# Score matmuls on stacked halves, gathers ahead of the dense loop, and three smaller reorderings in a two-block transformer kernel

## The chip, the cores and the metric

The kernel runs on one core of a Trainium2 chip. The metric is the device time of one execution in microseconds (us). The kernel before took 3409.3, 3415.68 and 3416.18 us in three runs, a median of 3415.68.

The engines have short names: PE is TensorE (matmuls), DVE is VectorE, ACT is ScalarE, POOL is GpSimd, SP is SyncE, which here only starts transfers. PSUM holds what PE adds up, SBUF everything else. Each engine runs its own instructions in order. A "FR" matmul is one on fp32r data, the form that PE takes in one pass; an fp32 matmul takes several.

## The reference, cut to what matters

Two blocks run one after the other, each of two layers, width D = 1024, on 256 latent tokens (and, in the first block's first layer, 256 context tokens beside them).

```python
# first block, each layer l:  mix (three branches, one of them attention), then PEER
q = apply_axial_rope(rmsnorm(q, q_norm[l]), ang_row, ang_col)      # 8 heads of 64
k = apply_axial_rope(rmsnorm(k, k_norm[l]), ang_row, ang_col)      # 2 heads of 64
k_all = concat([k, rmsnorm(kc, k_norm[l])])                        # latent and context keys
s = einsum('bqhgd,bkhd->bhgqk', q, k_all) * HEAD_DIM ** -0.5       # the scores
ya = softmax(s) @ v_all

def peer(h):                            # 8 heads, 128 x 128 = 16384 experts
    q = (h @ wq).reshape(C, 8, 2, 128)
    s = einsum('chpd,hpnd->chpn', q, sub_keys)
    s1, i1 = top_k(s[:, :, 0], 16); s2, i2 = top_k(s[:, :, 1], 16)
    top, pos = top_k(all 256 sums s1 + s2, 16)      # 16 experts of each head and token
    g = softmax(top)
    a = gelu(einsum('chkd,cd->chk', u_tab[eidx], h))
    return einsum('chk,chkd->cd', g * a, v_tab[eidx])

# second block, each layer: hybrid mixer, then memory cross attention
log_f = log_sigmoid(f_b + b_forget)     # forget gates: a few columns of the projection
dt    = softplus(dt_c + dt_bias)        # and as few more
xbc   = silu(causal_depthwise_conv(xbc_c, conv_w, conv_b))
```

## The kernel before

**Precision.** Nearly every fp32 operand is split into two fp32r parts, `hi` (an ACT cast, L128) and `lo` (a DVE subtraction of what is left, L129), and a product is three FR matmuls, hi·hi, hi·lo and lo·hi (`mm3`, lines 186 to 188 in the trace). Weights come through SP in tiles `raw` of 512 KB (5 buffers) and are split into `whi` and `wlo` (4 buffers).

**Order.** The code issues instructions in program order to a scheduler that places each engine's instructions by priority. What the engine then runs is a fixed list. `weave` interleaves generators, called units, in program order.

**Mix (L488 on).** For each token tile `qk_unit` norms, rotates and transposes q and k. q stays fp32, in `qT` with two heads of 64 rows on the 128 partitions. k is copied twice into `kT`, once for the upper and once for the lower head of a pair, and the other 64 rows are zeros that POOL wrote. `attn1_unit` then takes for each head one fp32 matmul of 128 queries by 512 keys (256 for the context queries). There are 24 units, each of two heads by 128 queries.

**PEER (L703 on).** All 16384 experts are not gathered for every token. The first 320 tokens in layer 0 (192 in layer 1) are "dense": for each of 128 chunks of 128 experts, `expert_in` multiplies the tokens by the chunk's u rows (24 FR matmuls) and makes G by gelu, a window `win` of routing weights multiplies it to `A`, `A` is split to `Ahl`, and 16 FR matmuls with the chunk's v rows add the result to PSUM. The other 192 (64) tokens are "gathered": for each of the 128 expert slots one indirect DMA brings the u and v rows of one slot for 128 tokens (`gat`, 1 MB, 4 buffers, on POOL's queue), DVE takes the dot product (L896), ACT the gelu (L897), and DVE adds to `gacc` (L908, L910) one gather later. With four buffers a gather waits until the one four ahead of it has been added.

Before the loop: queries and scores (`wq`), then the top 16 of each half and of their sums on DVE, then for each of four (layer 1: two) token tiles `route`, which turns positions into expert numbers `idx` (32 `pr` steps on DVE and PE) and writes the dense weights to DRAM (`wb` to `wd`). A number of `expert_in` run ahead of the loop (13 in layer 0, 30 in layer 1) to keep PE at work during the route. In the loop the n-th gather is placed by this rule:

```python
while gat and done < min(max(c - 5, 0) * ng // 119, ng):   # ng = 192 or 64
    done += 1
    with self.tc.issue_after(dma.ins), self.tc.issue_after(mul.ins):
        next(gat, None)
```

**Hybrid mixer (L1240 on).** First the forget gates and step sizes: a weight of 96 KB (`wfdr`, POOL's queue) is split, 24 matmuls give 24 columns (`fdT`), two transposes and an addition make `fd`. Then twelve `conv_unit`s are woven with the gate projections.

Of the kernel before, what the change touches and what calls it, by code (L numbers as in the profile page):

```python
# [9 lines left out]
F32 = mybir.dt.float32  # L10
# [34 lines left out]
def r3(ap, a):  # L45
    return ap.rearrange("p (a b) -> p a b", a=a)


class Net:
# [369 lines left out]

    def rope(self, out, src, cos, sin, nh, nb, f, pool):  # L420
# [11 lines left out]
        nc.vector.tensor_add(out, out, t[:, :w])  # L432

# [49 lines left out]
    def mix(self, l, both):  # L483
# [3 lines left out]
        with ExitStack() as es:  # L487
# [3 lines left out]
            hT = [ap.tile([128, 8, T], FR, name=n) for n in ("hTh", "hTl")]  # L491
            oT = [ap.tile([128, 4, TB], FR, name=n) for n in ("oTh", "oTl")]
# [4 lines left out]
            qT = bp.tile([128, 4, TB], F32, name="qT")  # L497
            kT = self.k_padded(bp, "kT", T)
            v = bp.tile([128, 4, 128], F32, name="v")
# [114 lines left out]
    def qk_unit(self, tp, rope, ps, t, gi, out, v):  # L614

        nc = self.nc
        cg, sg, kg = rope
        nh = 2 if gi else 8
        s = slice(t * 128, t * 128 + 128)
        q = self.headnorm(ps[:, :nh * 64], nh, tp)  # L620
        r = tp.tile([128, 512], F32, tag="qr", name="qr", bufs=3)[:, :nh * 64]
        if t < 2:
            self.rope(r, q, cg[:, gi, t], sg[:, gi, t], nh, 2, 16, tp)
        else:
            nc.vector.tensor_tensor(r3(r, nh), r3(q, nh), bc(kg[:, gi, None, :], [128, nh, 64]), op=OP.mult)
        if gi:
            self.evac(v[:, t], ps[:, 128:256])
        yield True
        if gi:
            self.k_put(out, r, tp, s)  # L630
            return
# [66 lines left out]
    def peer(self, l, both):  # L698
# [9 lines left out]
        with ExitStack() as es:  # L708
# [22 lines left out]
            with ExitStack() as e2:  # L731
                np_ = self.pool(e2, "wqp", side="right")
                scs, made = {}, []
                for cg in range(5):
                    qT = np_.tile([128, 4, 512], F32, tag="pq", name="pq", bufs=2) if cg < 4 else None
                    for c in range(4 if cg < 4 else 1):
                        if cg < 4:
                            ps = self.psum(c % 2)
                            self.proj_T(ps[:, :T], hT, i["wq"][l, cg * 4 + c], 0, T)
                            nc.scalar.copy(qT[:, c, :T], ps[:, :T])  # L740
                        if c == 0 and cg:
                            for t in range(NT):
                                ps = self.psum()
                                for k in range(4):
                                    nc.tensor.matmul(ps[:, k * 128:k * 128 + 128], pq[:, k, t * 128:t * 128 + 128], keys[:, k],
                                                     start=True, stop=True)
                                sc = scs[cg - 1, t] = np_.tile([128, 512], F32, tag="score", name="score", bufs=8)
                                nc.scalar.copy(sc, ps)
                    pq = qT
                    if cg < 4:  # L750
                        keys = np_.tile([128, 4, 128], F32, tag="keys", name="keys", bufs=2)
                        nc.gpsimd.dma_start(keys, i["keysT"][l, cg])
                    if cg:
                        for t in range(NT):
                            sc = scs[cg - 1, t]
                            for c in range(4):
                                n = (cg - 1) * 4 + c
                                self.top16(np_, sc[:, c * 128:c * 128 + 128], v16[t][:, n], i16[t][:, n], "tk")
                            self.candidates(np_, v16[t], top[t], pos[t], cg - 1)
            with ExitStack() as e2:  # L760
                rp = self.pool(e2, "rt", side="right")
                self.iota128 = rp.tile([128, 128], F32, name="iota128")
                nc.sync.dma_start(self.iota128, i["iota128"])
                self.iotah = rp.tile([128, 16, 8], FH, name="iotah")
                nc.vector.tensor_copy(self.iotah, r3(self.iota128, 16))
                if both:
                    self.mem_kv(0, range(GAPS["peer", 0][1].stop, 16), mp)
                for t in range(NT):
                    self.soft(rp, top[t])
                for t in range(NT):  # L770
                    g0 = (NT - 1 - t) * 128 if t * 128 + 128 > TD else 0
                    self.route(rp, top[t], pos[t], i16[t], t, l, wd, min(max(TD - t * 128, 0), 128), idx[:, g0:], gg[:, g0:])
# [7 lines left out]
            gp = self.pool(es, f"gp{l}", side="right")  # L780
            gat = self.gathered(gp, hT, idx, gg, TD, T) if ng else None
            nb = TD // 16
            ready = {}
            done = 0
            for c in range(128):
# [11 lines left out]
                ready[c] = ahl  # L797
                while gat and done < min(max(c - 5, 0) * ng // 119, ng):
                    done += 1
                    with self.tc.issue_after(dma.ins), self.tc.issue_after(mul.ins):  # L800
                        next(gat, None)
                if c == 125:
                    for _ in gat or ():
                        pass
# [142 lines left out]
    def route(self, rp, top, pos, i16, t, l, wd, nw, idx, gg):  # L947
# [21 lines left out]
        for a in range(2):  # L969
            for j in range(16):  # L970
# [239 lines left out]
    def hybrid(self, l):  # L1210
        nc, i = self.nc, self.i
        with ExitStack() as es:
# [32 lines left out]
            with ExitStack() as ec:  # L1245
                self.gap_fill("hybrid", l)
                self.normT(hT, "nm2T", l, bp)
                pp = self.pool(ec, f"hyp{l}", side="right")

                wr = pp.tile([128, 192], F32, name="wfdr")  # L1250
                nc.gpsimd.dma_start(wr, i["w2fd"][l])
                wf = [pp.tile([128, 192], FR, name=n) for n in ("wfdh", "wfdl")]
                self.split(wr, wf[0], wf[1])
                fdb = self.rowvec(pp, "fd_bias", 24, l)
                ps = self.psum()
                for k in range(8):
                    c = slice(k * 24, k * 24 + 24)
                    self.mm3(ps[:24, :256], (wf[0][:, c], wf[1][:, c]), (hT[0][:, k], hT[1][:, k]), k == 0, k == 7)
                fdT = pp.tile([24, 256], F32, name="fdT")
                nc.scalar.copy(fdT, ps[:24, :256])  # L1260
                for t in range(2):
                    nc.tensor.transpose(ps[:, 256 + t * 24:280 + t * 24], fdT[:, t * 128:t * 128 + 128], self.ident[:24, :24])
                nc.vector.tensor_tensor(fd, r3(ps[:, 256:304], 2), bc(fdb[:, None, :], [128, 2, 24]), op=OP.add)
                gates = self.hybrid_gates(l, hT, gT)
                self.weave((self.conv_unit(l, pp, hT, cw, m, xs, bcT) for m in range(12)), gates)
                for _ in gates:
# [30 lines left out]
            eb.close()  # L1297
        self.dump(f"x2_mix{l}", self.x)

    def hybrid_gates(self, l, hT, gT):  # L1300
# [373 lines left out]
```

## Time and profile before

| | us |
|---|---|
| three runs | 3409.3, 3415.68, 3416.18 |
| profiled execution | 3411.22 |
| its span in the trace | 3409.4 |
| PE busy (share of the span) | 3247.6 (95%) |
| DVE busy | 2598.9 (76%) |
| ACT busy | 1734.0 (51%) |
| POOL busy | 515.9 (15%) |

The stages, from the trace, in us from the span's start: modulation and the first mix to about 486; queries, top-k and route of the first PEER to 786; its dense loop to about 1742; second mix to about 1985; second PEER to about 2755; then hybrid, memory, hybrid, memory and the final norm. "Idle before" in a row is time in which an engine stood still, and the arrow names what ended it. A matmul's own length includes its way through the array, so what one costs is read from the distance between two starts. The granted clock (PEclk) is a share of 2.4 GHz, 0.50 being 1.2 GHz.

### The profile page before, as it was taken

The page shows a single profiled execution, that of the slowest core. Times are in us where ns is not written, and L with a number is a line of the kernel's source. Part 1 is how long each engine was busy: PE and PEld are TensorE (multiplying, and loading weights), DVE is VectorE, ACT ScalarE, POOL GpSimd, SP SyncE. Part 2 cuts the span into 40 slices and gives each one's busy share as a digit, 9 for nine tenths or more (in the row PEclk, how much of TensorE's full clock was granted, in tenths as well). Part 3 has the DMA queues.
Part 4 walks back from the last instruction along what each step waited for, and adds up shares of the span by engine and source line. Part 5 has one row for each costly group of instructions (what it writes and reads, how often), then busy time and mean ns, then how long its engine had stood idle before and what let it go on. Part 6 is the DMA issues. An engine that isn't in the chain of part 4 may idle for free.

```text
span 3409.4 us, 53017 instructions
## 1 busy us (share of the span) xinstructions
PE 3247.6 (95%) x19425; PEld 2779.9 (82%) x19425; DVE 2598.9 (76%) x5429; ACT 1734.0 (51%) x3711; POOL 515.9 (15%) x436
## 2 busy tenths in 40 slices
PE   8999999889999999999999998889999989999998
PEld 5666788768888888888877997769999989889887
DVE  3533449997989888999966678589999967755875
ACT  3443333385444444444444544557777745555554
POOL 0000000112333333333300000122222100000000
PEclk9999999889999999999999998999999999999999
DMA  6556232568999999999945555789999844255433
GB/s 244 193 194 219 88 128 80 173 177 312 377 398 379 378 381 372 379 392 389 390 158 173 166 178 170 267 340 389 372 370 377 346 159 161 93 189 174 142 120 109
DMA packets 196453, 860.52 MB, mean 252 GB/s; under 512 B 23920, under 2 KB 25664, under 8 KB 159712
## 3 DMA queue, kind: packets, MB, share of 16 engines
q1 hardware_dynamic: 141840, 505.94, 41.4%
q0 software_dynamic: 54352, 351.20, 26.8%
q8 instruction: 153, 2.51, 0.3%
q14 instruction: 108, 0.88, 0.1%
HBM read 816.15 MB, written 40.89 MB: 251 GB/s over the span
## 4 chain that ended last, share of the span: by engine, by line
PE 46%; issue 27%; DVE 12%; DMA 8%; POOL 6%; ACT 1%; POOLq 0%; DVEq 0%; SPq 0%; ACTq 0%
PE pf L188 5%; PE pf L186 5%; PE pf L187 5%; PE pf L860 4%; POOL gat L893 4%; PE ps L188 4%; PE ps L187 4%; PE ps L186 4%; DMA gat<-peer_uv,idx 4%; DVE wlo L129 3%; PE ps L824 3%; DVE gacc L910 2%; PE pf L859 2%; PE pf L370 1%; DMA wd<-wb 1%
## 5 line engine op out<-in xcount | busy, mean ns | idle before, releaser
L129 DVE TENSOR_TENSOR wlo<-raw,whi 128x1024 fp32r<-128x1024 f32 x778 | 940.1, 1219 | 388.2 <-ACT whi L128 378.2
L128 ACT CAST whi<-raw 128x1024 fp32r<-128x1024 f32 x778 | 814.4, 1047 | 572.8 <-PE pf L187 193.9
L893 POOL DMA_INDIRECT gat<-peer_uv,idx x256 | 406.2, 1587 | 917.3 <-DVE gacc L910 886.4
L188 PE MATMUL pf<-h2hl,wlo 128*128 128x320 f32 (+2 forms) x1152 | 368.6, 320 | 42.6 <-DVE wlo L129 42.5
L186 PE MATMUL pf<-h2hl,whi 128*128 128x320 f32 (+2 forms) x1152 | 367.2, 319 | 0.4 <-ACT mo L321 0.3
L187 PE MATMUL pf<-h2hl,whi 128*128 128x320 f32 (+2 forms) x1152 | 366.5, 318 | 0.0
L896 DVE SCALAR_TENSOR_TENSOR gat<-gat,h 128x1024 f32<-128x1024 f32 x256 | 311.5, 1217 | 70.2 <-DMA gat<-peer_uv,idx 69.8
L910 DVE SCALAR_TENSOR_TENSOR gacc<-gat,pga,gacc 128x1024 f32<-128x1024 f32 x253 | 322.9, 1276 | 0.0
L187 PE MATMUL ps<-wlo,Ahl 128*128 128x512 f32 x768 | 302.5, 394 | 6.2 <-DVE wlo L129 6.2
L186 PE MATMUL ps<-whi,Ahl 128*128 128x512 f32 x768 | 301.0, 396 | 4.1 <-ACT Ahl L128 4.1
L188 PE MATMUL ps<-whi,Ahl 128*128 128x512 f32 x768 | 301.6, 393 | 0.5 <-DVE Ahl L129 0.5
L188 PEld LDWEIGHTS pf<-h2hl,wlo 128*128 128x128 f32 x1152 | 221.9, 193 | 52.3 <-DVE wlo L129 49.6
L860 PE MATMUL pf<-h2hl,whi 128*128 128x384 f32 x784 | 238.5, 360 | 3.8 <-ACT whi L128 3.6
L186 PEld LDWEIGHTS pf<-h2hl,whi 128*128 128x128 f32 x1152 | 221.3, 192 | 8.1 <-ACT mo L321 0.5
L187 PEld LDWEIGHTS pf<-h2hl,whi 128*128 128x128 f32 x1152 | 221.4, 192 | 7.3
L128 ACT CAST Ahl<-A 128x320 fp32r<-128x320 f32 (+1 forms) x256 | 103.7, 405 | 218.1 <-DVE A L791 213.5
L859 PE MATMUL pf<-h2hl,wlo 128*128 128x192 f32 x686 | 174.9, 255 | 0.0
L188 PEld LDWEIGHTS ps<-whi,Ahl 128*128 128x128 f32 x768 | 145.0, 189 | 33.6 <-DVE Ahl L129 1.0
L187 PEld LDWEIGHTS ps<-wlo,Ahl 128*128 128x128 f32 x768 | 144.9, 189 | 31.0 <-DVE wlo L129 8.7
L186 PEld LDWEIGHTS ps<-whi,Ahl 128*128 128x128 f32 x768 | 144.9, 189 | 27.9 <-ACT Ahl L128 5.4
L897 ACT ACTIVATE pga<-pga 128x1 f32<-128x1 f32 x256 | 51.5, 201 | 226.1 <-DVE gat L896 225.7
L860 PEld LDWEIGHTS pf<-h2hl,whi 128*128 128x128 f32 x784 | 147.6, 188 | 8.6 <-ACT whi L128 4.4
(611 smaller groups left out, 7648.6 us busy)
## 6 DMA issues: line engine op xcount, KB each, us to landing
raw<-peer_uT SPq DMA_DIRECT2D x256, 512.0 KB
raw<-peer_v SPq DMA_DIRECT2D x256, 512.0 KB
raw<-ada_w SPq DMA_DIRECT2D x96, 512.0 KB
wd<-wb POOLq DMA_DIRECT2D x32, 1024.0 KB, 6.8
raw<-w_g SPq DMA_DIRECT2D x48, 512.0 KB
win<-wd POOLq DMA_DIRECT2D x16, 1280.0 KB, 9.5
raw<-wq SPq DMA_DIRECT2D x32, 512.0 KB
raw<-w2o SPq DMA_DIRECT2D x32, 512.0 KB
```

The costliest lines, as they stand in the source:

```text
L128: nc.scalar.copy(hi, src)
L129: nc.vector.tensor_sub(lo, src, hi.bitcast(F32))
L186: mm(ps, ah, bh, start=start, stop=False)
L187: mm(ps, ah, bl, start=False, stop=False)
L188: self.last = mm(ps, al, bh, start=False, stop=stop).ins
L824: nc.tensor.matmul(acc[nd][n], ahl[:, 2 * TD - part:], v[e][:, n], start=b == 0 and e == 0, stop=b == 127 and e == 1)
L859: mm(src, u[1][:, k], h2[:, k, 0, :TD], start=False, stop=False)
L860: self.last = mm(r3(ps[:, :2 * TD], 2), u[0][:, k], h2[:, k, :, :TD], start=k == 0, stop=k == 7).ins
L893: nc.gpsimd.indirect_dma_start(out=uv.rearrange("p a b -> p (a b)"), out_offset=None, in_=i["peer_uv"], in_offset=bass.IndirectOffsetOnAxi ...
L896: nc.vector.scalar_tensor_tensor(uv[:, 0], uv[:, 0], 1.0, h2, op0=OP.mult, op1=OP.mult, accum_out=a[:, 0:1])
L897: nc.scalar.activation(a[:, 1:2], a[:, 0:1], AF.Gelu_apprx_tanh)
L910: self.nc.vector.scalar_tensor_tensor(acc, uv[:, 1], a[:, 1:2], acc, op0=OP.mult, op1=OP.add)
```

## The change

There are five parts.

1. **Stacked scores.** q is duplicated before its transpose, so that each head stands twice on the 128 partitions; the upper 64 rows become the hi part, the lower 64 the lo part (one ACT copy that rounds, one DVE subtraction on the lower half). k is duplicated too and split into `kTh` and `kTl`. A score is then two FR matmuls, with kTh and with kTl, in place of one fp32 matmul. Eight heads need eight transposes where four pairs needed four. The attention's output takes qT's place, and the zeros of `kT` are gone.
2. **Queries and scores of layer 1** are all placed ahead of the top-k; layer 0 keeps its order.
3. **Softmax** over the 16 weights moves from ahead of all routes into each route, behind its `pr` steps.
4. **Early gathering, layer 0.** The gather's buffers open ahead of the `expert_in`s; six gathers are placed among the thirteen, and the other 186 are spread from chunk 2 to 124 where 192 stood from 5 to 124.
5. **Forget gates** become a unit that is joined to the third convolution.

```diff
-            for hh in range(2):  # attn1_unit
-            nc.tensor.matmul(ps[hh][:, :nk], qT[:, j, q0:q0 + 128], kT[:, hh, g, k0:k0 + nk], start=True, stop=True)
+            for n, k in enumerate(kT):
+                nc.tensor.matmul(ps[hh][:, :nk], qT[:, 2 * j + hh, q0:q0 + 128], k[:, g, k0:k0 + nk], start=n == 0, stop=n == 1)
...
-        pt = self.psum(True)  # qk_unit
-        for j in range(4):
-            nc.tensor.transpose(pt[:, j * 128:(j + 1) * 128], r[:, j * 128:(j + 1) * 128], self.ident)
-        self.evac(out[:, :, s], r3(pt, 4))
+        n = min(nh, 4)
+        for h0 in range(0, nh, n):
+            pt = self.psum(not gi)
+            for h in range(n):
+                nc.tensor.transpose(pt[:, h * 128:h * 128 + 128], r[:, h0 + h].rearrange("p a b -> p (a b)"), self.ident)
+            pt = r3(pt[:, :n * 128], n)
+            if gi:
+                self.split(pt, out[0][:, :, s], out[1][:, :, s])
+            else:
+                o = out[:, h0:h0 + n, s]
+                nc.scalar.copy(o, pt)
+                nc.vector.tensor_sub(o[64:128], pt[64:128], o[64:128].bitcast(F32))
...
+                made = [scores(cg) for cg in range(4)]  # peer
...
+                    if cg and both:
+                        best(cg - 1)
+                if not both:
+                    for cg in range(4):
+                        best(cg)
...
-                for t in range(NT):
-                    self.soft(rp, top[t])
...
-            gs = [self.expert_in(lp, l, c, h2, h32, TD, c < WHOLE[l]) for c in range(ahead)]
+            gp = self.pool(es, f"gp{l}", side="right")
+            gat = self.gathered(gp, hT, idx, gg, TD, T) if ng else iter(())
+            gs, g0 = [], 0
+            for c in range(ahead):
+                gs.append(self.expert_in(lp, l, c, h2, h32, TD, c < WHOLE[l]))
+                if both and c % 2:
+                    next(gat, None)
+                    g0 += 1
...
-            done = 0
+            done, c0 = g0, 2 if both else 5
-                while gat and done < min(max(c - 5, 0) * ng // 119, ng):
+                while done < min(g0 + max(c - c0, 0) * (ng - g0) // (124 - c0), ng):
...
+        self.soft(rp, top)  # route, behind the pr loop
...
+                us = [self.conv_unit(l, pp, hT, cw, m, xs, bcT) for m in range(12)]  # hybrid
+                us[2] = self.joined(self.fd_unit(l, pp, hT, fd), us[2])
+                self.weave(us, gates)
```

How the fixed lists move is read from the built programs.

POOL's queue at the end of layer 0's route, before (wd is the routing weights' write, win a window of them, gat a gather):

```order
L1032 DMA wd_3682<-wb 128x16x128 x12
L788 DMA win<-wd_3682 128x2560
L893 DMA gat<-peer_uv,idx 128x2048 x3
L788 DMA win<-wd_3682 128x2560
L893 DMA gat<-peer_uv,idx 128x2048
L788 DMA win<-wd_3682 128x2560
L893 DMA gat<-peer_uv,idx 128x2048 x13
```

and after:

```order
L1065 DMA wd_3735<-wb 128x16x128 x12
L925 DMA gat<-peer_uv,idx 128x2048 x6
L820 DMA win<-wd_3735 128x2560
L925 DMA gat<-peer_uv,idx 128x2048 x3
L820 DMA win<-wd_3735 128x2560
L925 DMA gat<-peer_uv,idx 128x2048 x6
L820 DMA win<-wd_3735 128x2560
L925 DMA gat<-peer_uv,idx 128x2048 x12
```

The first window now stands behind six gathers and the second behind nine, and each later window has 12 or 13 gathers before the next, where nearly all had 13.

DVE behind the expert numbers of the last routed tile (idx), before:

```order
L993 CAST idx<-ef 128x128
L129 TENSOR_TENSOR wlo<-raw,whi 128x1024 x3
L791 TENSOR_TENSOR A<-G,win 128x320
L129 TENSOR_TENSOR wlo<-raw,whi 128x1024
...
L887 TENSOR_TENSOR hs<-h2hl 128x128 x2
L129 TENSOR_TENSOR wlo<-raw,whi 128x1024
L896 SCALAR_TENSOR_TENSOR gat,pga<-gat,h_7874 128x1024 x3
```

and after:

```order
L1026 CAST idx<-ef 128x128
L919 TENSOR_TENSOR hs<-h2hl 128x128 x8
L928 SCALAR_TENSOR_TENSOR gat,pga<-gat,h_7448 128x1024
L129 TENSOR_TENSOR wlo<-raw,whi 128x1024
L940 TENSOR_SCALAR gacc<-gat,pga 128x1024
...
L928 SCALAR_TENSOR_TENSOR gat,pga<-gat,h_7448 128x1024
L942 SCALAR_TENSOR_TENSOR gacc<-gat,pga,gacc 128x1024
L129 TENSOR_TENSOR wlo<-raw,whi 128x1024
L823 TENSOR_TENSOR A<-G,win 128x320 x2
```

Before, thirteen splits of weights (wlo) and eight products with windows (A) stood ahead of the first gather's use; now six gathers are used ahead of the first product with a window, each with a split behind it. On PE the matmuls of `expert_in` that stand behind the route's last matmul grow from 186 to 264.

PE at the start of the first hybrid mixer, before (wfdh and wfdl are the forget gates' weights, h3h and h3l the normed tokens):

```order
L262 MATMUL ps<-dg,x 128x128 x13
L186 MATMUL pf<-h3h,whi 128x256
...
L188 MATMUL pf<-h3h,wlo 128x256
L186 MATMUL ps<-h3h,wfdh 24x256
L187 MATMUL ps<-h3l,wfdh 24x256
L186 MATMUL ps<-h3h,whi 128x256
L188 MATMUL ps<-h3h,wfdl 24x256
```

and after:

```order
L262 MATMUL ps<-dg,x 128x128 x13
L186 MATMUL ps<-h3h,whi 128x256
...
L1220 MATMUL ps<-ident,cacc 128x128 x2
L186 MATMUL pf<-h3h,whi 128x256
...
L186 MATMUL ps<-h3h,wfdh 24x256
L187 MATMUL ps<-h3l,wfdh 24x256
L188 MATMUL ps<-h3h,wfdl 24x256
L186 MATMUL ps<-h3h,whi 128x256
```

Before, 24 matmuls of a gate stood between the normed tokens and the forget gates; now 48 of two gates, 48 of two convolutions and two transposes stand there.

## Rows read from the trace of the kernel before

**Rows 1.** The page: engines in 40 slices, tenths busy; DMA is 16 engines' share.
```profile
PE   8999999889999999999999998889999989999998
...
DMA  6556232568999999999945555789999844255433
```
**Rows 2.** Timeline of PE in the first mix: start, us, engine, line, operation, operands, count.
```profile
211.05 0.40 PE L188 MATMUL pf<-hTh,wlo 128*128 128x512 f32 x1
211.28 0.39 PE L186 MATMUL pf<-hTh,whi 128*128 128x512 f32 x1
...
219.96 1.98 PE L645 MATMUL ps<-kT,qT 128*128 128x512 f32 x4
221.88 1.09 PE L660 MATMUL ps<-pT,v 128*64 128x128 f32 x16
```
**Rows 3.** The score line L645: all its matmuls, min/median/max ns, first and last start.
```profile
L645 PE MATMUL ps<-kT,qT x96: 379/592/697, 137.4 to 1888.7; 128*128 128x512 f32 x64, 128*128 128x256 f32 x32
```
**Rows 4.** Timeline of PE in the second mix.
```profile
1830.92 0.66 PE L634 MATMUL pf<-ident,qr 128*128 128x128 f32 x4
...
1854.99 0.28 PE L188 MATMUL pf<-hTh,wlo 128*128 128x256 f32 x1
1855.11 0.29 PE L186 MATMUL pf<-hTh,whi 128*128 128x256 f32 x1
```
**Rows 5.** Windows of both mixes: stretch, us, PE, PEld, DVE, ACT, POOL busy, PEclk, DMA share, GB/s.
```profile
120.00:130.00 10.00, 9.20 (x52) 6.47 (x50) 8.29 (x27) 4.32 (x14) 0.00 (x0) 1.00 0.30 103
1860.00:1880.00 20.00, 20.00 (x170) 17.01 (x167) 12.24 (x31) 14.46 (x30) 0.00 (x0) 1.00 0.35 106
```
**Rows 6.** DVE's copies of a transposed q tile in the first mix.
```profile
L121 DVE COPY qT<-pf x4: 684/690/692, 112.7 to 125.1; 128x512 f32<-128x512 f32 x4
```
**Rows 7.** The page's group of DVE's split subtraction: busy us, mean ns, idle before.
```profile
L129 DVE TENSOR_TENSOR wlo<-raw,whi 128x1024 fp32r<-128x1024 f32 x778 | 940.1, 1219 | 388.2 <-ACT whi L128 378.2
```
**Rows 8.** Windows of layer 0's route, its dense loop, and the loop's start.
```profile
650.00:786.00 136.00, 113.45 (x986) 84.99 (x985) 124.29 (x319) 108.59 (x272) 26.26 (x26) 0.86 0.64 190
...
850.00:1700.00 850.00, 815.53 (x4463) 734.15 (x4462) 775.58 (x1002) 404.22 (x922) 294.41 (x195) 0.99 0.98 383
...
816.00:846.00 30.00, 30.00 (x135) 24.22 (x134) 25.41 (x42) 14.96 (x34) 8.39 (x6) 1.00 0.76 293
```
**Rows 9.** Transfers in 850 to 1700: issues, KB each, median us to landing.
```profile
raw<-peer_v SPq DMA_DIRECT2D x113, 512.0 KB
...
gat<-peer_uv,idx POOLq DMA_INDIRECT x182, 9.4
```
**Rows 10.** Waits in 850 to 1700: who for whom, us in total, times, longest.
```profile
POOL gat L893 <- DVE gacc L910: 534.2, 178, 7.6
...
PE pf L188 <- DVE wlo L129: 33.7, 19, 4.1
```
**Rows 11.** Timeline of PE over one chunk of the dense loop, v matmuls to v matmuls.
```profile
1004.43 0.40 PE L186 MATMUL ps<-whi,Ahl 128*128 128x512 f32 x1
...
1011.19 0.31 PE L186 MATMUL pf<-h2hl,whi 128*128 128x320 f32 x1
...
1011.63 0.40 PE L186 MATMUL ps<-whi,Ahl 128*128 128x512 f32 x1
```
**Rows 12.** Timeline of POOL's queue: the fifth gather of layer 0.
```profile
833.17 1.69 POOL L893 DMA_INDIRECT gat<-peer_uv,idx  x1 [7.76 <-DVE gacc L908]
```
**Rows 13.** Timeline of PE at the first hybrid mixer.
```profile
2776.18 0.41 PE L186 MATMUL ps<-h3h,wfdh 128*24 128x256 f32 x1 [3.65 <-ACT wfdh L128]
```
**Rows 14.** The same place on ACT.
```profile
2775.78 0.35 ACT L128 CAST wfdh<-wfdr 128x192 fp32r<-128x192 f32 x1 [4.67 <-DMA wfdr<-w2fd]
```
**Rows 15.** Windows: behind that place, and among layer 1's top-k.
```profile
2776.00:2782.00 6.00, 5.82 (x28) 4.52 (x29) 1.58 (x2) 3.00 (x5) 0.00 (x0) 0.50 0.68 249
...
2046.00:2052.00 6.00, 1.29 (x9) 1.09 (x9) 6.00 (x32) 1.32 (x2) 0.00 (x0) 0.97 0.00 0
```
**Rows 16.** A wait of DVE behind layer 1's route.
```profile
DVE A L791 <- DMA win<-wd: 16.4, 1, 16.4
```

More of the change, by code (lines that the diff above doesn't have):

```diff
@@ L418, in headnorm, with rope @@
         return qn[:, :w]
-    def rope(self, out, src, cos, sin, nh, nb, f, pool):
+    def rope(self, out, src, cos, sin, nh, nb, f, pool, add=None):
         nc = self.nc
@@ L491, in mix @@
             hT = [ap.tile([128, 8, T], FR, name=n) for n in ("hTh", "hTl")]
-            oT = [ap.tile([128, 4, TB], FR, name=n) for n in ("oTh", "oTl")]
+            qT = ap.tile([128, 8, TB], FR, name="qT")
+            oT = [qT.rearrange("p (j n) t -> p n j t", n=2)[:, n] for n in range(2)]
             pscale = ap.tile([128, 2], F32, name="pscale")
@@ L496, in mix @@
             bp = self.pool(eb, f"mixb{l}")
-            qT = bp.tile([128, 4, TB], F32, name="qT")
-            kT = self.k_padded(bp, "kT", T)
+            kT = [bp.tile([128, 2, T], FR, name=n) for n in ("kTh", "kTl")]
             v = bp.tile([128, 4, 128], F32, name="v")
@@ L732, in peer @@
                 np_ = self.pool(e2, "wqp", side="right")
-                scs, made = {}, []
-                for cg in range(5):
[L735 to L741, printed above, removed]
-                            for t in range(NT):
[L743 to L749, printed above, removed]
+                scs = {}
@@ new lines, in scores @@
+                def scores(cg):
+                    qT = np_.tile([128, 4, 512], F32, tag="pq", name="pq", bufs=2)
+                    keys = np_.tile([128, 4, 128], F32, tag="keys", name="keys", bufs=2)
+                    nc.gpsimd.dma_start(keys, i["keysT"][l, cg])
+                    for c in range(4):
+                        ps = self.psum(c % 2)
+                        self.proj_T(ps[:, :T], hT, i["wq"][l, cg * 4 + c], 0, T)
+                        nc.scalar.copy(qT[:, c, :T], ps[:, :T])
+                        yield
+                    for t in range(NT):
+                        ps = self.psum()
+                        for k in range(4):
+                            nc.tensor.matmul(ps[:, k * 128:k * 128 + 128], qT[:, k, t * 128:t * 128 + 128], keys[:, k],
+                                             start=True, stop=True)
+                        sc = scs[cg, t] = np_.tile([128, 512], F32, tag="score", name="score", bufs=8)
+                        nc.scalar.copy(sc, ps)
@@ L750, in peer, with best @@
+                def best(cg):
+                    for t in range(NT):
+                        sc = scs[cg, t]
+                        for c in range(4):
+                            n = cg * 4 + c
+                            self.top16(np_, sc[:, c * 128:c * 128 + 128], v16[t][:, n], i16[t][:, n], "tk")
+                        self.candidates(np_, v16[t], top[t], pos[t], cg)
+                made = [scores(cg) for cg in range(4)]
+                for cg in range(5):
                     if cg < 4:
-                        keys = np_.tile([128, 4, 128], F32, tag="keys", name="keys", bufs=2)
@@ L752, in peer @@
-                        nc.gpsimd.dma_start(keys, i["keysT"][l, cg])
+                        next(made[cg])
                     if cg:
[L754 to L759, printed above, removed]
+                        for _ in made[cg - 1]:
+                            pass
@@ L760, in peer @@
+                    for _ in range(3 if cg < 4 else 0):
+                        next(made[cg])
+                    if cg and both:
[3 more added lines that the diff above has]
+                        best(cg)
             with ExitStack() as e2:
@@ L768, in peer @@
                 for t in range(NT):
-                    self.soft(rp, top[t])
-                for t in range(NT):
                     g0 = (NT - 1 - t) * 128 if t * 128 + 128 > TD else 0
@@ L802, in peer @@
                 if c == 125:
-                    for _ in gat or ():
+                    for _ in gat:
                         pass
@@ L1248, in hybrid @@
                 pp = self.pool(ec, f"hyp{l}", side="right")
[L1250 to L1263, printed above, removed]
                 gates = self.hybrid_gates(l, hT, gT)
-                self.weave((self.conv_unit(l, pp, hT, cw, m, xs, bcT) for m in range(12)), gates)
+                us = [self.conv_unit(l, pp, hT, cw, m, xs, bcT) for m in range(12)]
+                us[2] = self.joined(self.fd_unit(l, pp, hT, fd), us[2])
+                self.weave(us, gates)
                 for _ in gates:
@@ L1298, in hybrid, with joined, fd_unit @@
         self.dump(f"x2_mix{l}", self.x)
+    @staticmethod
+    def joined(a, b):
+        next(a, None)
+        yield from b
+        for _ in a:
+            pass
+    def fd_unit(self, l, pp, hT, fd):
+        nc, i = self.nc, self.i
+        wr = pp.tile([128, 192], F32, name="wfdr")
+        nc.gpsimd.dma_start(wr, i["w2fd"][l])
+        wf = [pp.tile([128, 192], FR, name=n) for n in ("wfdh", "wfdl")]
+        self.split(wr, wf[0], wf[1])
+        fdb = self.rowvec(pp, "fd_bias", 24, l)
+        ps = self.psum()
+        for k in range(8):
+            c = slice(k * 24, k * 24 + 24)
+            self.mm3(ps[:24, :256], (wf[0][:, c], wf[1][:, c]), (hT[0][:, k], hT[1][:, k]), k == 0, k == 7)
+        fdT = pp.tile([24, 256], F32, name="fdT")
+        nc.scalar.copy(fdT, ps[:24, :256])
+        yield True
+        for t in range(2):
+            nc.tensor.transpose(ps[:, 256 + t * 24:280 + t * 24], fdT[:, t * 128:t * 128 + 128], self.ident[:24, :24])
+        nc.vector.tensor_tensor(fd, r3(ps[:, 256:304], 2), bc(fdb[:, None, :], [128, 2, 24]), op=OP.add)
     def hybrid_gates(self, l, hT, gT):
```

17 lines of the change are left out of this document (8 added, 9 removed).

## The prediction

> **What bounds the kernel now.** I read the page first, then one stretch for each part of the change. The page [rows 1] shows two regimes. In most slices PE is at 9 tenths with DMA at 2 to 6; there a microsecond off PE is a microsecond off the end. In the dense loop of layer 0 PE and DMA both stand at 9, and which of them ends it decides what early gathering is worth.
>
> In both mixes PE is never short of work once the attention runs: 20.00 of 20 us busy at a granted clock of 1.00, with DVE at 12.24 and ACT at 14.46 [rows 5]. Only where q and k are made are PE (9.20 of 10) and DVE (8.29) both nearly full.
>
> In the dense loop one chunk takes PE 7.20 us from v matmuls to v matmuls when it does not wait (1011.63 − 1004.43) [rows 11]. There were 113 chunks in 850 us by the v issues [rows 9], so a chunk took 7.52. The 33.7 us that PE waited for split weights [rows 10] are most of the difference. DMA is at 0.98 for those 850 us, moving 383 GB/s [rows 8]. So transfers pace the loop, and PE keeps some 0.3 us in a chunk, about 36 us over the loop, in reserve. That gathers wait 534.2 us for gacc [rows 10] is the closed ring of four buffers, not a lack of DVE time (775.58 of 850).
>
> **Part 1, scores.** One unit of the 512-key kind takes 221.88 − 219.96 = 1.92 us for two heads [rows 2]. It becomes four FR matmuls of 512 columns at 211.28 − 211.05 = 0.233 us, 0.93 together: 0.99 saved. A 256-key unit has half the columns: 0.96 for two heads, against four matmuls of 0.12 (1855.11 − 1854.99) [rows 4], 0.48 saved. The 64 long and 32 short records [rows 3] are four to a unit, 16 and 8 units. 16 × 0.99 + 8 × 0.48 = 19.7 us less on PE, 12 in the first mix and 8 in the second.
>
> Added on PE: six q tiles with four more transposes each. Four took at most 0.66 us [rows 4], so 24 × 0.145 = 3.5 us (0.145 between that row's two bounds, 0.11 and 0.165). Net −16.2.
>
> The transposes run in a stretch whose granted clock is 1.00 [rows 5], the upper level. The Trainium skill, "TensorE: Matmul & The Clock Gate", section "Part 4: PE-mode transpose", says that a transpose doesn't count as PE activity the way a matmul does, and gives about 275 ns in one kernel's context. By that figure the 24 would cost an estimated 6.6 us and this part would be −13.1; the spacing in this trace is half of it and stands.
>
> Added on DVE, for each of the six q tiles: the last rope step (or the gain) writes 1024 columns in place of 512, and two subtractions from PSUM on 64 partitions take the place of one copy of 512 columns. With 0.69 us for a 512-column operation [rows 6] and 1.219 for 1024 [rows 7] that is 0.53 + 0.69 = 1.2 us a tile, 7.3 in all. For k, the doubling is paid by the copy that goes. DVE has 1.7 us of 10 free there [rows 5]. If all shows, part 1 is −8.9; if none, −16.2. I take a quarter, since DVE's 8.29 leaves it room but its order is fixed: **−14.4**.
>
> **Part 5, forget gates.** PE stands still for 3.65 us because ACT's cast of wfdh ended last [rows 13], and the cast waited 4.67 us for its 96 KB [rows 14]. Behind the pause the granted clock is 0.50: 28 matmuls took 5.82 us [rows 15], 0.208 each in place of 0.12, 2.5 lost. The 48 gate and 48 convolution matmuls that now stand in front are 96 × 0.12 = 11.5 us of work with weights that have their own buffers, so the 96 KB are there in time. Next late is nothing I can see: the conv's splits were ready before. −3.65 − 2.5 = **−6.2**; the bounds are 0 (another weight late in its place) and −7.
>
> **Part 4, early gathering.** Three effects.
> First, three `expert_in`s' ACT and DVE work (each a gelu, a cast, a subtraction) leaves the route, where DVE is busy 124.29 of 136 us and ACT 108.59 [rows 8]. 3 × 1.2 us of DVE splits [rows 7] make the route about 3 us shorter.
> Second, their 78 matmuls at 0.147 us ((1011.63 − 1011.19) / 3) [rows 11], 11.5 us, now come behind the route. PE's reserve of about 36 us swallows that if transfers still end the loop.
> Third, the transfers. From 816 to 846 DMA stands at 0.76 [rows 8], so 30 × 0.24 = 7.2 us idle: the fifth gather waits until 833.17 for the first to be added [rows 12]. With the gathers used ahead of A, most of that fills; I take 5. Against it, two u tiles fewer have been loaded by the route's end, 1.05 MB at 383 GB/s, 2.7 us. Bytes in all are the same: 3 + 5 − 2.7 gives **−5**. The bounds: −10 if the whole idle time goes and the u tiles cost nothing; +8.5 if PE's 11.5 shows in full against the route's 3.
>
> The Trainium skill, "DMA: Bandwidth & Descriptors", section "Anatomy of one DMA — SWDGE (gpsimd) path", fits a transfer to 2.0 us and 436 GB/s. By it, as an estimate, a chunk's 2.88 MB (383 GB/s × 7.52 us) pass in 6.6 us, under PE's 7.20; PE would end the loop and the sum would be the first rival's. The trace disagrees: 383 GB/s at a share of 0.98, and 9.4 us from issue to landing of a gather.
>
> **Parts 2 and 3.** Layer 1's PE has 1.29 busy us in 2046 to 2052 [rows 15], where a query's weight split stood among the top-k on DVE; ten splits come earlier now. But DVE is full there (6.00 of 6), the top-k keeps its length, and behind the route a window's load is last (16.4 us) [rows 16]. So what PE gains becomes waiting. The softmax only moves, in layer 0 to a place where DVE and ACT are as busy; in layer 1 it comes ahead of the casts that the routing waits for, 1 to 2 us late. **−1** for both, bounds −4 and +4.
>
> **Sum.** −14.4 − 6.2 − 5 − 1 = −26.6 on the profiled 3411.2 gives 3384.6. That execution lies 4.5 us under the median of its three runs (3415.7) and 1.9 above the fastest; between them I say **3386 us**. By the ends the sum runs from −37 to +4.
>
> **Rivals.**
> *PE ends the loop.* DMA's 0.98 would be a queue that is always full, not a ceiling. For it: PE is busy 815.53 of 850 us [rows 8]. Against: it waited for weights all the same [rows 10]. Then part 4 is +8.5, the rest stands: −13, **3399**.
> *The loop falls to PE's pace.* Gathers per chunk go from 192/119 = 1.61 to 186/122 = 1.52, 0.09 MB less, at 383 GB/s 0.24 us a chunk; if the early gathers cost nothing, 112 × 0.24 = 27 us go, a chunk takes 7.28, near PE's 7.20. For it: 0.24 of idle share at the loop's start. Against: that is 7 us of room, and six gathers of 1.05 MB need 16. Then part 4 is about −25: −46, **3366**.
> *Slower: DVE stands before early gathers.* A gather needs 9.4 us to land [rows 9]; its use now stands on DVE ahead of a weight split that PE needs. With four split buffers PE has 4 × 3.5 = 14 us of work in hand at the route's end, so the first wait hides; but the fifth and sixth gather start only when the first and second have been added, and land 9.4 us later. If each of the six holds PE, and half the clock follows each pause as in rows 15, six times 5.5 us is 33. It decides from there, 33 against the 26.6: **3424**. Against it: each stall also lets transfers run ahead, and the reserve swallows 36.
> *The score doesn't gain*, because softmax on DVE and ACT sets the attention's pace: against it stand 12.24 and 14.46 of 20 [rows 5]. Then −12, near the first rival, **3400**.
>
> **How the numbers follow.** My forecast has 0.56; PE ending the loop 0.15, the score without gain 0.07, PE's pace 0.13, slower 0.09. The likeliest one's own range, with the bounds of its unknowns half used, is 3374 to 3398. The range for 8 in 10 takes in PE's pace and both middle rivals with their spread: 3363 to 3407. A measurement of this kernel can tell 0.2%, 6.8 us, from no change. Faster: the forecast, PE's pace, and most of the two middle rivals, 0.82. Within: the rest of those, 0.10. Slower: 0.08.
>
> **What would show it.** Right: L657 in place of L645 with four matmuls in about 0.93 us and the second mix some 7 us shorter; no pause at the first wfdh, its window at 1.00; in 816 to 846 a DMA share of 0.9; a loop that ends some 5 us earlier against the route's start, DMA still at 0.98. Wrong: in the loop PE without waits (first rival); DMA's share falling under 0.95 (second); PE idle several times between the route's end and the first A, with DVE's gat waiting for its DMA (third); DVE at 10 of 10 while q is made and PE standing beside it (part 1 at its upper bound).

## The result and the profile after

The changed kernel takes 3371.97 us (median of four runs, 3367.91 to 3373.43) where the kernel before takes 3414.68: a ratio of 0.9876, 95% interval 0.9859 to 0.9893, 42.7 us less. The forecast was 3386 us, 26.6 less on the profiled execution; the time lies in its range of 3363 to 3407. The profiled executions differ by 3411.22 − 3371.84 = 39.4 us, and the stages show where. One execution of spread_only below, at 5407.1 us and a mean granted clock of 0.645, is left out of that kernel's ratio.

Three marks cut the span: the last expert numbers of layer 0 (idx), and the updates of x behind the mixes (upd) and behind the dense loops (gat). For each instruction group the rows give ns min/median/max and the first and last start; the first start of upd and of gat belongs to layer 0, the last to layer 1. Before:

```profile
L584 DVE TENSOR_TENSOR x<-x,upd x8: 681/682/692, 444.6 to 1987.5; 128x512 f32<-128x512 f32 x8
L837 DVE TENSOR_TENSOR x<-x,gat x8: 682/688/694, 1743.1 to 2757.4; 128x512 f32<-128x512 f32 x8
```
```profile
L993 DVE CAST idx<-ef x1: 216/216/216, 786.2 to 786.2; 128x128 int32<-128x128 f32 x1
```

and after:

```profile
L589 DVE TENSOR_TENSOR x<-x,upd x8: 684/685/693, 436.6 to 1955.7; 128x512 f32<-128x512 f32 x8
L869 DVE TENSOR_TENSOR x<-x,gat x8: 681/688/695, 1718.5 to 2722.4; 128x512 f32<-128x512 f32 x8
```
```profile
L1026 DVE CAST idx<-ef x1: 226/226/226, 778.8 to 778.8; 128x128 int32<-128x128 f32 x1
```

The first mix ends 8.0 us earlier (444.6 to 436.6). From there to the expert numbers nothing is won: 341.6 us before, 342.2 after. The dense loop of layer 0 takes 939.7 us (778.8 to 1718.5) in place of 956.9, 17.2 less. The second mix takes 237.2 in place of 244.4, 7.2 less. Layer 1's PEER is 3.2 us shorter, and what follows it 4.3 (span 3370.1 against 3409.4).

The page's slices, after, answer to [rows 1]:

```profile
PE   8999999879899999999999997989999999999998
...
DMA  6566232569999999999944555889999854255432
```

The picture is the same: PE and the transfers at 9 in the dense loops, PE with the transfers well below it elsewhere. What changed shows only in rows with finer numbers.

The scores gain a little less than computed. The timeline of PE in the first mix, after, answers to [rows 2]:

```profile
176.44 0.50 PE L657 MATMUL ps<-kTh,qT 128*128 128x512 f32 x1
176.78 0.39 PE L657 MATMUL ps<-kTl,qT 128*128 128x512 f32 x1
177.00 0.39 PE L657 MATMUL ps<-kTh,qT 128*128 128x512 f32 x1
177.23 0.39 PE L657 MATMUL ps<-kTl,qT 128*128 128x512 f32 x1
177.55 1.09 PE L672 MATMUL ps<-pT,v 128*64 128x128 f32 x16
```

A unit goes from 1.92 us to 177.55 − 176.44 = 1.11: the first of the four stands 0.34 from the second, not 0.23, and the next instruction 0.32 behind the last. In the second mix a unit goes from 1.81 (1850.63 to 1852.44) to 1.03 (1823.43 to 1824.46), and a 256-key unit of the first from 1.06 (262.38 to 263.44) to 0.66 (244.58 to 245.24).

The dense loop is where the forecast was small. These are the windows 900 to 1650 (us, then busy us and instructions of PE, PEld, DVE, ACT, POOL, PEclk, DMA share, GB/s), the issues of v tiles and gathers in them, and before's one wait of PE there. Before:

```profile
900.00:1650.00 750.00, 720.98 (x3955) 649.87 (x3954) 684.49 (x885) 358.10 (x817) 260.45 (x172) 0.99 0.98 385
```
```profile
raw<-peer_v SPq DMA_DIRECT2D x99, 512.0 KB
gat<-peer_uv,idx POOLq DMA_INDIRECT x160, 9.2
```
```profile
PE pf L188 <- DVE wlo L129: 29.0, 16, 4.1
```

After:

```profile
900.00:1650.00 750.00, 750.00 (x4143) 674.16 (x4142) 693.98 (x897) 380.21 (x836) 264.94 (x169) 1.00 0.99 390
```
```profile
raw<-peer_v SPq DMA_DIRECT2D x104, 512.0 KB
gat<-peer_uv,idx POOLq DMA_INDIRECT x157
```

In the same 750 us there are 104 chunks in place of 99, 7.21 us each, which is PE's own pace of [rows 11]; PE waits for nothing. DMA's share is 0.99 against 0.98, but it moved 390 GB/s against 385. So a chunk took 2.92 MB before and 2.81 MB after; by these two rates, as an estimate, the fewer bytes account for 0.27 of the 0.36 us that a chunk got shorter, and the higher rate for the rest.

What PE's waits hung on is seen on DVE, which makes the split weights: before, it stood still for 65.5 of the 750 us, nearly all of it ahead of gathers that had not landed. After, that wait is a third, though DVE did more work (693.98 us for 684.49). Before and after:

```profile
DVE gat L896 <- DMA gat<-peer_uv,idx: 60.9, 33, 6.1
```
```profile
DVE gat L928 <- DMA gat<-peer_uv,idx: 17.7, 15, 2.4
```

The loop's start filled up too: 816 to 846 had 293 GB/s at 0.76 [rows 8]; the same window has 396 GB/s at 1.00 after, where the forecast's sign was a share of 0.9. Two windows around it, after:

```profile
810.00:840.00 30.00, 30.00 (x160) 26.51 (x160) 28.35 (x39) 16.53 (x40) 7.21 (x6) 1.00 1.01 414
840.00:870.00 30.00, 24.66 (x108) 19.95 (x108) 25.59 (x37) 12.27 (x30) 10.30 (x8) 0.94 0.91 352
```

Behind the filled stretch PE stands for 5 of 30 us. That is not a price of the early gathers: the kernel before stands about as long in the same window.

```profile
840.00:870.00 30.00, 25.27 (x119) 21.33 (x118) 27.86 (x38) 13.13 (x33) 10.34 (x8) 0.95 0.95 349
```

POOL's timeline, after, shows how the six are issued, against [rows 12]:

```profile
779.89 1.07 POOL L925 DMA_INDIRECT gat<-peer_uv,idx  x1 [3.87 <-PE pf L920]
...
790.11 1.97 POOL L925 DMA_INDIRECT gat<-peer_uv,idx  x1 [4.68 <-DMA gat<-peer_uv,idx]
794.00 1.67 POOL L925 DMA_INDIRECT gat<-peer_uv,idx  x1 [1.92 <-DVE gacc L942]
795.68 0.61 POOL L820 DMA_DIRECT2D win<-wd  x1
```

The fifth gather starts at 790.1, 11.3 us behind the expert numbers, where it started 47 us behind them (833.17 − 786.2).

### The profile page after: what moved, and what is told of

It reads as the page before. It is cut to its first block, busy times and chain, and to the rows that moved or that the text cites. A ratio compares the mean times of both kernels' runs of the same rounds, so it can differ in the third digit from the quotient of the medians.

```text
span 3370.1 us, 53059 instructions
## 1 busy us (share of the span) xinstructions
PE 3230.3 (96%) x19449; PEld 2775.4 (82%) x19449; DVE 2607.3 (77%) x5430; ACT 1748.3 (52%) x3720; POOL 519.6 (15%) x432
## 5 line engine op out<-in xcount | busy, mean ns | idle before, releaser
L925 POOL DMA_INDIRECT gat<-peer_uv,idx x256 | 413.8, 1616 | 918.8 <-DVE gacc L942 875.2
L186 PE MATMUL pf<-h2hl,whi 128*128 128x320 f32 (+2 forms) x1152 | 362.7, 315 | 0.2 <-ACT mo L321 0.2
L187 PE MATMUL pf<-h2hl,whi 128*128 128x320 f32 (+2 forms) x1152 | 361.8, 314 | 0.0
L187 PE MATMUL ps<-wlo,Ahl 128*128 128x512 f32 x768 | 305.4, 398 | 10.5 <-DVE wlo L129 10.4
L856 PE MATMUL ps<-wlo,Ahl 128*128 128x512 f32 x384 | 151.4, 397 | 0.0
```

Source lines behind the costliest of these rows:

```text
L186: mm(ps, ah, bh, start=start, stop=False)
L187: mm(ps, ah, bl, start=False, stop=False)
L856: nc.tensor.matmul(acc[nd][n], ahl[:, 2 * TD - part:], v[e][:, n], start=b == 0 and e == 0, stop=b == 127 and e == 1)
L925: nc.gpsimd.indirect_dma_start(out=uv.rearrange("p a b -> p (a b)"), out_offset=None, in_=i["peer_uv"], in_offset=bass.IndirectOffsetOnAxi ...
```

## Experiments

All were profiled. The times are medians against the kernel before on the same chip. They scatter more than the stages do, so the stages are set side by side first (us, from each profile, cut at the same marks; "behind" is all that follows layer 1's last gather update):

| | first mix | to idx | dense loop 0 | second mix | PEER 1 | behind |
|---|---|---|---|---|---|---|
| before | 444.6 | 341.6 | 956.9 | 244.4 | 769.9 | 652.0 |
| changed | 436.6 | 342.2 | 939.7 | 237.2 | 766.7 | 647.7 |
| changed_again | 437.9 | 343.0 | 940.2 | 239.0 | 766.3 | 647.7 |
| b_only_scores | 437.4 | 341.8 | 959.2 | 239.4 | 767.1 | 649.8 |
| a_gathers_undone | 436.4 | 343.7 | 959.5 | 238.1 | 774.8 | 648.4 |
| a_softmax_undone | 435.3 | 343.0 | 944.7 | 240.5 | 772.6 | 649.4 |
| a_gates_undone | 435.6 | 344.4 | 943.0 | 239.8 | 767.3 | 649.2 |
| queries_undone | 436.5 | 343.2 | 940.9 | 238.7 | 766.4 | 647.8 |
| spread_only | 435.6 | 347.3 | 944.0 | 237.7 | 770.1 | 649.7 |
| early_only | 434.8 | 343.3 | 948.1 | 239.6 | 768.8 | 647.5 |
| early_twelve | 436.8 | 346.9 | 958.1 | 237.9 | 768.2 | 647.9 |
| before_24_fewer | 447.4 | 343.4 | 909.0 | 242.4 | 764.9 | 646.9 |
| changed_24_fewer | 437.1 | 343.4 | 933.3 | 239.3 | 764.8 | 648.4 |
| paced_gathers | 436.7 | 346.5 | 939.8 | 239.5 | 767.9 | 651.8 |

PEER 1 goes from 764.8 to 774.8 among kernels whose code for it hardly differs. Its 3.2 us of the result are not told from scatter. The stage "to idx" goes from 341.6 to 347.3; where it is longer, PE can do work in it that would else stand in the loop, so two loops are compared safely only with that stage taken in.

**b_only_scores.** The kernel before with the diff's hunks on `rope`, `mix`, `qk_unit` and `attn1_unit` alone.

```diff
-            nc.tensor.matmul(ps[hh][:, :nk], qT[:, j, q0:q0 + 128], kT[:, hh, g, k0:k0 + nk], start=True, stop=True)
+            for n, k in enumerate(kT):
+                nc.tensor.matmul(ps[hh][:, :nk], qT[:, 2 * j + hh, q0:q0 + 128], k[:, g, k0:k0 + nk], start=n == 0, stop=n == 1)
```

> The kernel before with part 1 alone (stacked scores). My theory, by the starts of the stages in the two traces (first mix 8.0 us shorter, second mix 7.2): about 15 us faster than before, 3399 to 3401. Rival: the shorter mixes come partly from other parts (the order of layer 1's queries, the pools), and part 1 alone gives under 10. Second rival: what PE saves there is lost again in the dense loop of layer 0, where transfers pace the work and start no earlier: then only the second mix's 7 are left.

3403.41 us, ratio 0.997 (0.9956 to 0.9985): 9.5 us by the medians, 14.7 by the spans of the profiled pair. The medians fall short of the 3399 to 3401 expected, and their interval, 5 to 15 us, does not separate the theory from its first rival; the stages do. The mixes are 7.2 and 5.0 us shorter with part 1 alone, and the dense loop is not (959.2). Part 1 gives some 12 us here, at its place, and the second rival, that the dense loop takes the first mix's gain back, is not borne out beyond the 2 us by which that loop is longer.

**a_gathers_undone.**

```diff
-                if both and c % 2:
-                    next(gat, None)
-                    g0 += 1
...
-            done, c0 = g0, 2 if both else 5
+            done, c0 = g0, 5
```

> The changed kernel with part 4 undone (gathers as before: none ahead of the loop, 192 from chunk 5 to 124). Theory: part 4 alone is the 17 us by which layer 0's dense loop got shorter, so 3387 to 3391, PE waits for split weights in the loop again (30 us or more) and a chunk takes 7.5 us again. Rival: the loop got shorter because parts 1 to 3 let it start in another state; then under 8 us are lost.

3397.87 us, ratio 0.9955 (0.9942 to 0.9968), 7 us slower than the 3387 to 3391 expected. The dense loop is back at 959.5, and PE's wait is back:

```profile
PE pf L188 <- DVE wlo L129: 27.1, 15, 3.6
```

With b_only_scores that gives three loops without part 4 (956.9 to 959.5) and five with it (939.7 to 944.7). Part 4 is worth 12 to 20 us there, 17 in the result's pair, and no other part brings it.

**a_softmax_undone.** `soft` again ahead of all routes.

```diff
+                for t in range(NT):
+                    self.soft(rp, top[t])
...
-        self.soft(rp, top)
```

> The changed kernel with part 3 undone (softmax of all tiles ahead of all routes). Theory: the softmax only moves within a stretch where DVE is full, so no difference that can be told, within 3 us of 3372. Rival: it is what made layer 1's route 1.8 us longer, so this version is 2 us faster; or what made room at the top-k's end, then it is 3 us slower.

3381.53 us, ratio 0.9896 (0.9872 to 0.9921). Against the changed kernel's 0.9876 and (changed_again) 0.9896 it can't be told apart; layer 0's way to the expert numbers is unchanged (343.0). Inconclusive for a microsecond or two, as the forecast's size was.

**a_gates_undone.**

```diff
-                us[2] = self.joined(self.fd_unit(l, pp, hT, fd), us[2])
```
(and the forget gates ahead of the convolutions as before)

> The changed kernel with part 5 undone (forget gates ahead of the convolutions). Theory: the pause of 3.7 us and the half clock behind it come back, 5 us slower in the first hybrid mixer, and the second mixer gains 0.8 us: 3376 to 3378. Rival: the pause was a matter of when the dense loop ended against POOL's queue and SP's loads; in the changed kernel the 96 KB come in time all the same and nothing is lost.

3379.67 us, ratio 0.9904 (0.9879 to 0.9929), not told apart by time; the stage behind PEER 1 is 1.5 us longer than in the changed kernel, where 5 were expected. That is within the scatter of this stage among kernels that all have part 5 (647.5 to 651.8). The pause is back, but not what I had priced behind it. PE's timeline at the forget gates:

```profile
2748.26 0.30 PE L186 MATMUL ps<-h3h,wfdh 128*24 128x256 f32 x1 [3.22 <-ACT wfdh L128]
2748.39 0.28 PE L187 MATMUL ps<-h3l,wfdh 128*24 128x256 f32 x1
```

The matmuls stand 0.13 apart, not 0.21: the granted clock stayed at 1.00. In b_only_scores (pause 3.37) and before_24_fewer (3.43) it stayed there too. Only in the profiled execution of before (3.65) [rows 13, 15] was it at 0.50.

**changed_again, spread_only, early_only, early_twelve**, together on another chip.

> The changed kernel once more, beside the next three on one chip: 3372, within 5 us; layer 0's dense loop (from the last expert numbers to the first update of x) 937 to 946 us.

3378.66 us, ratio 0.9896 (0.9881 to 0.9911); the loop takes 940.2. The time is 1.7 us above the range expected, and the whole change is worth 37.1 us here, where the result had 42.7.

```diff
-                if both and c % 2:
+                if both and c < 0:      # spread_only
```

> The changed kernel without the six early gathers: all 192 spread from chunk 2 to 124 (1.57 a chunk, in place of six and 1.52). Theory (what counts is the megabytes moved in the first 60 us behind the route, where DMA was idle): most of part 4's gain goes, the dense loop takes 951 to 957 us and PE waits for split weights through the whole loop. Rival (the lower number of gathers per chunk is enough to bring the loop to PE's pace of 7.20): the loop stays under 946.

3386.21 us, ratio 0.9913 (0.9898 to 0.9929). By the loop alone the rival, under 946: 944.0. But the way to the expert numbers is 5.7 us longer than before (347.3 for 341.6). Both stages together take 1291.3, against 1298.5 before and 1281.9 in the changed kernel: starting at chunk 2 in place of 5, with fewer gathers a chunk (1.57 for 1.61), brings 7 of 17 us, and PE's wait in 900 to 1650 falls to half:

```profile
PE pf L188 <- DVE wlo L129: 13.5, 12, 2.5
```

```diff
-            done, c0 = g0, 2 if both else 5
+            done, c0 = g0, 5      # early_only
```

> The changed kernel with the six early gathers but the others from chunk 5 on as before (1.56 a chunk). Theory (early megabytes): about half of the gain is kept, the dense loop takes 945 to 950 us. Rival (the spread matters): 953 or more.

3378.62 us, ratio 0.9888 (0.9873 to 0.9904). 948.1, as my theory had it, with 10.1 us of that wait. With the stage ahead of it, 1291.4: 7 of 17 us again. So by the stages each half brings about half, though by the medians there is no difference between this kernel and the changed one (3378.66); what the later start adds to the six is not shown in the time.

```diff
-                if both and c % 2:
+                if both and c:          # early_twelve
```

> The changed kernel with twelve early gathers, one behind each of the thirteen expert_ins but the first, in place of six. Theory (PE's pace of 7.20 a chunk now ends the loop): nothing more to gain, the dense loop takes 937 to 946 us and DMA's share falls a little towards the loop's end. Rival (transfers still end it): 6 x 2.7 = up to 16 us more gained. Second rival (DVE stands before gathers that haven't landed, and the windows' products behind it): slower, 950 us or more, with PE idle between the route's end and the first v matmul.

3388.69 us, ratio 0.9924 (0.991 to 0.9937). The second rival, which is also my forecast's way to slower: 958.1, all of part 4's gain lost. The first window is issued behind the twelfth gather on POOL, 29 us later than with six (25 by the distance from the expert numbers), and PE stands before the first v matmul:

```profile
823.48 1.68 POOL L925 DMA_INDIRECT gat<-peer_uv,idx  x1 [1.80 <-DVE gacc L942]
825.15 0.61 POOL L820 DMA_DIRECT2D win<-wd  x1
```

```profile
PE ps L186 <- ACT Ahl L128: 11.2, 1, 11.2
```

**before_24_fewer, changed_24_fewer.** In layer 0 every eighth gather is left out, with its part of the result.

```diff
             for s in range(s0, s0 + w):
+                if t1 == 512 and s % 8 == 7:
+                    continue
...
-                while gat and done < min(max(c - 5, 0) * ng // 119, ng):   # before; in the changed kernel likewise
+                while gat and done < min(max(c - 5, 0) * (ng * (7 if both else 8) // 8) // 119, ng):
```

> The kernel before with 24 of layer 0's 192 gathers left out (every eighth slot's contribution is missing from the result; the rest spread over the same chunks, 1.41 a chunk). Theory (transfers pace the loop of before, PE has about 35 us of waits and half clock in it): the dense loop loses those and no more, 957 becomes 915 to 925 us, and PE's waits for split weights almost vanish. Rival (PE's waits come from the fixed order on DVE, not from bytes): under 15 us less.

3363.19 us, ratio 0.9843 (0.9816 to 0.9871). 909.0, 48 us less, more than the 32 to 42 I gave; PE is never without work in the window:

```profile
900.00:1650.00 750.00, 750.00 (x4168) 679.47 (x4168) 671.72 (x866) 378.86 (x817) 250.41 (x159) 1.00 0.96 374
```

> The changed kernel with the same 24 gathers left out. Theory (PE's pace now ends the loop): hardly anything to gain, the dense loop takes 928 to 940 us where it took 940, and DMA's share falls to about 0.9. Rival (transfers still end it): 24 x 1.05 MB at 391 GB/s are 64 us, of which 25 or more would show.

3365.17 us, ratio 0.9846 (0.9816 to 0.9876). 933.3, 7 less; DMA has room, and nothing becomes of it:

```profile
900.00:1650.00 750.00, 750.00 (x4143) 674.17 (x4142) 647.44 (x834) 373.48 (x793) 238.40 (x150) 1.00 0.94 361
```

This pair settles the loop. The same 24 transfers less are worth 48 us to the kernel before and 7 to the changed one: transfers paced the first, PE paces the second. Leaving out a gather also takes its work off DVE, which no run separates; but DVE's wait for gathers that have not landed fell with it from 60.9 us to 10.1, and the changed kernel lost PE's waits with more work on DVE, not less. And where PE waits for no weights in 900 to 1650, the kernel before has the shorter loop, by 24 us. In the 340 us ahead of the expert numbers its PE ran 2037 matmuls, the changed kernel's 1952; the 85 that come later, 78 of them those of the three expert_ins by the fixed lists, cost some 12 us at 0.147. From the expert numbers to 900 PE stands 5.1 us in place of 2.3. The rest of the 24 I have not taken apart.

**queries_undone.**

```diff
-                    if cg and both:
+                    if cg:
                         best(cg - 1)
-                if not both:
-                    for cg in range(4):
-                        best(cg)
```

> The changed kernel with part 2 undone (layer 1 takes the top-k of a group behind the next group's queries again). Theory: the pause of PE among the top-k (4.7 us) comes back, but DVE's top-k keeps its length, and the route and the dense loop of layer 1 together change by less than 3 us. Rival: the earlier queries are what made layer 1's dense loop 5 us shorter, so 5 us slower.

3378.86 us, ratio 0.9891 (0.9863 to 0.9919). PEER 1 takes 766.4 against 766.7 and 766.3: nothing, as expected.

**paced_gathers.**

```diff
-                while done < min(g0 + max(c - c0, 0) * (ng - g0) // (124 - c0), ng):
+                x, n = (4 * (c - 2) - min(max(c - 2, 0), 11), 477) if both else (c - 22, 102)
+                while done < min(g0 + max(x, 0) * (ng - g0) // n, ng):
```

> The changed kernel with the gathers paced by what a chunk costs: in layer 0 three quarters of the rate for the first chunks, whose expert_in is already done, and in layer 1 the gathers from chunk 22 on instead of 5. Theory (PE waits 840 to 900 in layer 0 and 2180 to 2300 in layer 1 because short chunks ask for u, v and gathers faster than 390 GB/s): layer 1's dense loop loses 4 to 8 us of its 601, layer 0's 0 to 4 of its 940. Rival (bytes put off come back as waits at the end): no gain in either, or layer 0 slower by up to 8.

3376.25 us, ratio 0.9868 (0.9842 to 0.9894). The rival: 939.8 and 767.9, no gain. 840 to 900 is full now, but in 900 to 1650 PE waits again, 7.3 us for split weights, as if the bytes put off came back.

## Why the prediction was right, and where not

The time lies in the range, but not wholly by the forecast's own path. The sum was 26.6 us and the profiled pair differs by 39.4. Nearly all of the gap is part 4: there a rival came true to which I had given 0.13, and the range holds because it was drawn to take that rival in.

*What bounds the stages:* right for the kernel before, wrong for the one after. PE bound the mixes, and transfers paced the dense loop of the kernel before (before_24_fewer shows it; it was read from DMA's 0.98 and PE's waits). That transfers would still end the loop after the change was wrong (changed_24_fewer).

*Part 1, −14.4:* the total is right, 15.2 by the stages of the profiled pair, 12 to 16 in the other profiles; its terms are not. A long unit saves about 0.8 us in both mixes, not 0.99, and a short one 0.40, not 0.48. I had measured the unit before up to the next instruction's start, and the unit after as four bare spacings. So the scores give 16 × 0.81 + 8 × 0.40 = 16.2 in place of 19.7, and less the 3.5 for the transposes 12.7. The 1.8 us charged for DVE's added work would make it 10.9; the mixes lost more than that in every profile, so no such charge shows. What the pair has beyond 12.7 I have not accounted for. That the total came out at 14.4 is in part luck: two misses of opposite sign.

*Part 5, −6.2:* too large. It is −4.3 behind PEER 1 in the profiled pair, 1.5 against a_gates_undone, which differs in it alone, and neither is clear of that stage's scatter. The pause itself goes, and the granted clock is 1.00 at the first wfdh, as forecast. But the half clock behind the pause came in one of the four profiled kernels that have the pause, and a new wait appeared where I saw nothing late: ACT still stands 3.7 us before the 96 KB, now with a convolution's work behind it, and PE waits 1.31 us for that.

```profile
2744.66 0.44 PE L1220 MATMUL ps<-ident,cacc 128*128 128x128 f32 x2 [1.31 <-ACT cacc L1216]
```

*Parts 2 and 3, −1:* nothing, as near as can be told.

*Part 4, −5, is the step that failed:* 17 were measured. "Make the route about 3 us shorter" was wrong: taking three splits from DVE in a stretch where it is busy 124 of 136 us moved the route's end by nothing (341.6 to 342.2). That PE's reserve would swallow the 11.5 held in that the loop got shorter all the same; but the reserve is now spent, and PE paces the loop. The mis-sized term is the third: I filled 7.2 us of idle DMA, held the bytes and their rate fixed, and so could not get below the old pace. In fact 28 gathers were issued within 122 us of the expert numbers, where 22 had been, and with 1.52 gathers a chunk PE ran through at 7.21 while DMA carried 390 in place of 385 GB/s. This is the second rival, "the loop falls to PE's pace", which I gave 0.13 and sized at −25; the 17 measured are nearer to it than to my 5. The argument I held against it, that 7 us of room can't take six gathers of 1.05 MB, counted room at 0.98 share as none. The signs I had named did not tell the rivals apart either: PE without waits in the loop, meant for the first rival, came without that rival's 8.5 us of loss, and DMA's share falling under 0.95, meant for the second, did not come (0.99).

The 436 GB/s of the Trainium skill ("DMA: Bandwidth & Descriptors", "Anatomy of one DMA — SWDGE (gpsimd) path") are not what the loop reaches: it has 390, and 414 in the fullest 30 us shown.

*The rival on the slower side* was real, only at another number: with twelve in place of six it takes all of part 4's gain. I had put its point of decision at 5.5 us for each of six; with six PE had expert_ins in hand until the window came, with twelve it had not. Its price, 3424, also drops part 4's 5 us without saying so; 33 against 26.6 alone give 3419.

## What to carry to other kernels

Where two engines stand within a few per cent of each other, a loop can pass from one's pace to the other's, and what a change is worth is the distance to the second pace, as far as it removes load, and not the idle time that it fills. To know which paces it, take a known load off one of them and see whether the time follows. A penalty seen once in one profile, like a clock that fell behind a pause, is a price only if other executions show it.

## What the runs showed of the hardware that I had not expected

The granted clock fell to 0.50 behind a pause of PE of 3.65 us in one execution, and stayed at 1.00 behind pauses of 3.43, 3.37 and 3.22 us at the same place in three others. A DMA share of 0.98 to 0.99 went with 382 to 390 GB/s in the dense loop, and one of 1.01 with 414 in 30 us at the loop's start. A share near 1 thus stood beside rates 8% apart, and beside a loop that transfers paced as well as one that they did not.
